# Token-major v made once per layer by whole 128x128 transposes, and the outputs' products grouped by array shape, in the RWKV mixers of a four-layer network

## The chip, the cores and the metric

The kernel runs on one core of one Trainium2 chip. The metric is the device time of one execution in microseconds (us).

## What is computed

Four layers in a row on 512 latent tokens of 1024 channels; the first two carry 256 context tokens along. Each of the first two layers projects its normalised input and gives the parts to three mixers: an RWKV mixer (4 heads of 64 channels, run over the tokens forwards and backwards), a short convolution and differential attention. The last two layers, attention and a gated recurrence, each with a feed-forward part, are not touched here. The RWKV part of the reference, cut:

```python
def rwkv_scan(state0, terms, reverse, with_output):
    def step(S, inp):
        w_t, k_t, v_t, a_t, b_t = inp[-5:]
        sa = jnp.einsum('bhvk,bhk->bhv', S, a_t)
        S = S * w_t[:, :, None, :] + sa[..., None] * b_t[:, :, None, :] + v_t[..., None] * k_t[:, :, None, :]
        y_t = jnp.einsum('bhvk,bhk->bhv', S, inp[0]) if with_output else None
        return S, y_t
...
    for d, reverse in ((0, False), (1, True)):
        s_ctx, y_c = rwkv_scan(state0, tc, reverse, need_ctx_out)
        _, y_l = rwkv_scan(s_ctx, tl, reverse, True)
```

`need_ctx_out` holds in the first layer only.

## The kernel before

The RWKV scan is done in chunks of 64 tokens. `layer` calls `rw_stage` six times per layer: three blocks of 256 tokens (context first) for each of two directions `d`. One stage, in the order of the code:

1. It loads its slices of keys, r and (in `rw_vt`) v from DRAM, where the projections left them channel-major.
2. *Preparation*: decay and rate from two small products with `wup` (L528), a scan and exponentials on ScalarE and VectorE, then the tiles `G` and `AR`; the in-chunk products `AS` (L584), masked by VectorE; the transposes `GT` of `G` (L595).
3. `rw_vt` turns v token-major, 16 blocks of 64x64: even heads' blocks by TensorE's transpose mode, odd heads' as plain float32 products with the identity (L504; a plain float32 product shows as two instructions in the trace, a transpose as one, so a stage has 24).
4. The diagonal blocks of the chunk matrices are inverted: `AS` goes through DRAM into a layout of one block per partition, VectorE does 15 serial steps (L613 to L617, tiles `X`, `tt`), and the result returns through DRAM into `D` and `DT` by 16 small transfers (L627). Then `txA` (L636, tile `tx`), a mask into `W` (L637), and three rounds of `tx` products (L645) with an addition each give `TT`.
5. *Chunks*: for each of four chunks, `zp` from `AS`, `UV` and the running state (L664 and L666), copied to `zs`; `up` from `TT` and `zs` (L673), copied into `UV`; `sp` from `GT` and `UV` (L681), from which VectorE makes the next state (L686, L687); and the output `yp`, for each of four heads one product with `UV` (L695, all 128 rows and 64 columns of the array, written 128*64 below) and one with the state (L697, 64*64). `UV` holds v and `up` stacked.

The projections that are still missing (`proj`, products L324) have no tie to the stages and stand between them. The Tile scheduler sets the order on each engine when the program is built, from its own estimates of durations; each engine then works through its list in order. Most of a stage's tiles have one buffer (`rb` = 1: `G`, `X`, `D`, `DT`, `W`, `vt`), those of the chunks two (`cb` = 2: `AR`, `AS`, `GT`, `TT`, `UV`). The two stages of one block of the order (d = 0, then d = 1) are prepared close together, so that there are three *pairs* of stages per layer. A *burst of v* below is one stage's L504 group.

Of the kernel before, what the change touches and what calls it, by code (L numbers as in the profile page):

```python
# [19 lines left out]
P = 128  # L20
# [29 lines left out]
# ---------------------------------------------------------------- host layout  # L50
# [105 lines left out]
def _wt(w, nk=8):  # L156
    """[K, N] -> [N/128, K/(128*nk) pieces, 128, nk, 128]"""
    K, N = w.shape
    return np.ascontiguousarray(w.reshape(K // (P * nk), nk, P, N // P, P).transpose(3, 0, 2, 1, 4))


def prep(inputs):
# [4 lines left out]
    # [l, nblk 6, 128, 8, 512]  # L167
# [11 lines left out]
    # f(rel) = rb[rel + 383]; table row p, column m: rel = p - m + 384  # L179
# [3 lines left out]
    g = np.stack([a["rg_w_a_2"][0], a["rg_w_i_2"][0]], 1)  # [blk, 2, 256, 256]  # L183
    o["rgg"] = np.ascontiguousarray(g.reshape(4, 2, 2, P, 256).transpose(0, 3, 1, 2, 4))  # blk, p, gate, kc, col
# [30 lines left out]
# ---------------------------------------------------------------- kernel  # L215
class Kern:
    def __init__(self, es, tc, ins, out, dbg=None, upto=99):
# [11 lines left out]
        # a load that the following weight loads queue up behind  # L229
        self.behind = self.last_load = None  # L230
        # GpSimd takes the low parts of every so many weights (0: of none)
# [19 lines left out]
    def mm(self):  # L251
        """a bank of products: of self.pm, or of two pools in turn"""
        pool, n = self.pm, self.nmm
        if self.mms:
            pool, n = self.mms[self.nmms % len(self.mms)]
            self.nmms += 1
        return self.t(pool, [P, 512], "mm", n)

    # ---- persistent state
# [24 lines left out]
    # ---- weights  # L284
    def load_w(self, src, nk=8, ncol=P, keep=None):
        """src: dram AP [128, nk, ncol] -> (hi, lo) float32r tiles; keep: (pool, number) of tiles apart from the rolling ones"""
# [16 lines left out]
    def split(self, hi, lo, src, eng=None):  # L303
        """hi + lo = src, both float32r"""
# [3 lines left out]
    def put_split(self, dst, cols, src, hi):  # L308
        """high and low part of src to dram; hi: scratch; src is overwritten"""
# [5 lines left out]
    def gemm(self, ps, wl, mov, total=None):  # L315
        """ps: list of psum APs, wl: list of (hi, lo, nk); mov: list (per psum) of function kc -> (hi, lo)"""
# [16 lines left out]
    def order(self, later, first):  # L333
        """first before later in their engine's queue"""
        self.tc.add_manual_dep(later.ins, first.ins.name, mybir.DependencyInfo(mybir.DependencyClass.NoSync, mybir.DependencyReason.DATA), reason="order")

    # ---- reciprocal square roots
    def rsqrt_cols(self, pool, src, n, eps=None, floor=None):
        """1 / sqrt(src + eps) of [128, n] (n small): bit-level seed and three Newton steps"""
# [15 lines left out]
    def log_tables(self):  # L355
        """the tables of rsqrt_act (and of Exp, Square, Copy, Identity), ahead of its first use"""
        self.tc.keep_in_program_order(self.nc.scalar.preload_act_table_set("natural_log_exp_and_others"))

    def rsqrt_act(self, pool, src, n, eps=EPS, half=False):
        """1 / sqrt(src + eps) of [128, n] (n small, eps: number or [128, n]): seed from the logarithm and one Newton step"""  # L360
# [20 lines left out]
    def tok_sum(self, ps, sqs, n, hold=None):  # L381
        """ps[token, b] = sum over channels (partitions, and the tiles of sqs) of token block b; hold: so many columns of later products come first"""
# [7 lines left out]
    def tok_sum2(self, st, sq, i):  # L390
        """as tok_sum, one tile after the other; only the very first product has the start flag, which clears the whole bank"""
# [10 lines left out]
    def bcast(self, pool, ps, cols, nb):  # L402
        """ps[:, token] (psum, nb * 128 columns) = cols[token, block] on every partition"""
# [7 lines left out]
    def heads_bcast(self, pool, ps, cols):  # L411
        """ps[channel, token] of one 128-channel chunk = cols[token, head of the channel]"""
# [5 lines left out]
    # ---------------------------------------------------------------- rwkv  # L418
    def rw_alloc(self, l, es):
        """tiles and small per-partition coefficients of one layer's rwkv mixer"""  # L420
# [3 lines left out]
        for n in ("r", "v", "m0", "m1", "ks0", "ks1", "ys0", "ys1"):  # L424
            R[n] = self.dp.tile([P, 2, T], F32, tag=f"rw{n}_{l}", name=f"rw{n}_{l}", bufs=1)
        R["lw"] = self.t(rp, [P, T], "lw")
# [5 lines left out]
        # 0:4 w0/2, 4:8 a0/2, 8:10 kk0, 10:12 kk1, 12:14 al(k), 14:16 be(k), 16:18 alpha0, 18:20 beta0, 20:22 alpha1, 22:24 beta1  # L432
# [9 lines left out]
        # slot 0: even rows k, odd rows b (alpha = beta = -0.5, negated) ; slot 1 the other way round  # L442
# [4 lines left out]
        # static buffers of the block inverses  # L447
# [16 lines left out]
    def rw_keys(self, l, ks, st):  # L464
        """m0 = [k even ; kk odd], m1 = [kk even ; k odd]; ks: sbuf tiles of k per channel chunk"""
# [27 lines left out]
    def rw_vt(self, tb):  # L493
        """token-major v of one token block: even heads in rows 0:64, odd heads in rows 64:128"""
        nc, R, rp = self.nc, self.R, self.rp
        ident = self.c("ident")
        ps = self.t(self.pa, [P, 8, 64], "ax", self.nax)
        vt = self.t(rp, [P, 8, 64], "vt", self.rb)
        vl = self.rw_load("v", tb, 1)
        for c in range(4):  # L500
            for hp in range(2):
                for e in range(2):
                    h = slice(e * 64, e * 64 + 64)
                    nc.tensor.matmul(ps[h, c * 2 + hp, :], lhsT=vl[h, hp, c * 64:c * 64 + 64], rhs=ident[h, h],  # L504
                                     start=True, stop=True, is_transpose=e == 0)
        nc.scalar.copy(out=vt, in_=ps)
        return vt

    def rw_stage(self, l, d, st, with_y):
# [10 lines left out]
        rl = self.rw_load("r", tb, 1) if with_y else None  # L520

        # decay and in-context rate
# [1655 lines left out]
```

## Time and profile before

| | |
|---|---|
| runs shown | 2908.32, 2912.96, 2920.25 us (median 2912.96) |
| profiled execution, first to last instruction | 2921.2 us |
| TensorE busy | 2677.0 us (92%) |
| VectorE, ScalarE, GpSimd busy | 1528.2, 1034.2, 743.2 us |
| the two RWKV mixers, by the places of their stages' products | 146 to 492 us, and 991 to 1355 us |

TensorE is busy most of the time, but its matmuls overlap: one that shows 0.22 us can begin 0.04 us after the one before it. What a group costs is therefore read from where it begins and where the next group begins, not from its busy time. `PEclk` is the granted clock of TensorE in a stretch, as a share of 2.4 GHz; at 0.50 it is at its lower level, 1.2 GHz, throughout.

### The profile page before, as it was taken

To read this page: it belongs to the slowest core of one execution; us is meant where nothing else is said; L and a number is where in the kernel's file an instruction comes from. 1 tells how busy PE (TensorE), PEld (TensorE's weight loads), DVE (VectorE), ACT (ScalarE), POOL (GpSimd) and SP (SyncE) were. 2 spreads that over 40 slices of the span, in tenths; PEclk is the share of its full clock that TensorE was granted. 3 is DMA by queue.
4 is the path that set the end of the run, shared out by engine and by line. 5 is a ranking of instruction groups with operands and counts; after the bars stand their busy time and mean duration, and the time that the engine had idled before them with its cause. 6 is when DMAs were issued, how large, how long until landed. Compare 5 with 4: busy or idle time off the path is not lost.

```text
span 2921.2 us, 42875 instructions
## 1 busy us (share of the span) xinstructions
PE 2677.0 (92%) x16938; PEld 2171.6 (74%) x16938; DVE 1528.2 (52%) x2925; ACT 1034.2 (35%) x1946; POOL 743.2 (25%) x631
## 2 busy tenths in 40 slices
PE   5999999969988999999898999799999987999998
PEld 2877777756687766666667888698888876988886
DVE  7264553517644366464375666665443487654423
ACT  4231222216534222122254445543222356432221
POOL 2310111414445121112122325431110254411101
PEclk8988979978798878889789999899999998999999
DMA  5332223466232322224643111022223311222232
GB/s 200 124 98 56 57 77 106 145 177 187 89 130 86 103 68 66 77 72 133 195 129 112 44 62 51 22 73 94 94 94 93 99 55 65 87 94 95 94 99 74
DMA packets 173785, 283.31 MB, mean 97 GB/s; under 512 B 53648, under 2 KB 110864, under 8 KB 173584
## 3 DMA queue, kind: packets, MB, share of 16 engines
q1 hardware_dynamic: 173584, 280.58, 31.0%
q8 instruction: 133, 2.18, 0.3%
q14 instruction: 68, 0.56, 0.1%
HBM read 235.68 MB, written 44.83 MB: 96 GB/s over the span
## 4 chain that ended last, share of the span: by engine, by line
PE 57%; DVE 13%; ACT 5%; issue 4%; POOL 3%; DMA 3%; SPq 0%; POOLq 0%; ACTq 0%; DVEq 0%
PE mm L324 14%; PE mm L1495 7%; PE mm L1458 5%; PE mm L1456 5%; PE mm L1459 5%; PE mm L1562 2%; PE s L1149 2%; PE s L1148 2%; DVE tt L616 1%; POOL wlo L300 1%; PE po L1194 1%; ACT whi L297 1%; PE ax L504 1%; PE tx L645 1%; PE yp L697 1%
## 5 line engine op out<-in xcount | busy, mean ns | idle before, releaser
L297 ACT CAST whi<-wraw 128x1024 fp32r<-128x1024 f32 (+2 forms) x311 | 318.2, 1026 | 702.3 <-PE mm L1458 281.1
L300 POOL TENSOR_TENSOR wlo<-wraw,whi 128x1024 fp32r<-128x1024 f32 (+1 forms) x122 | 292.9, 2403 | 830.4 <-ACT whi L297 753.8
L1458 PEld LDWEIGHTS mm<-hlo,whi 128*128 128x128 f32 x1632 | 311.8, 191 | 75.1
L1456 PE MATMUL mm<-hhi,whi 128*128 128x512 f32 x816 | 330.1, 404 | 9.5 <-ACT whi L297 9.5
L324 PE MATMUL mm<-hhi,whi 128*128 128x512 f32 (+1 forms) x992 | 331.2, 370 | 3.9 <-ACT whi L297 2.1
L1459 PE MATMUL mm<-hhi,wlo 128*128 128x512 f32 x816 | 327.1, 401 | 6.2 <-POOL wlo L300 6.2
L1458 PE MATMUL mm<-hlo,whi 128*128 128x256 f32 x1632 | 330.2, 284 | 0.0
L324 PE MATMUL mm<-hlo,whi 128*128 128x512 f32 (+1 forms) x992 | 327.6, 365 | 0.5 <-POOL hlo L843 0.5
L300 DVE TENSOR_TENSOR wlo<-wraw,whi 128x1024 fp32r<-128x1024 f32 (+1 forms) x189 | 235.0, 1246 | 177.3 <-ACT whi L297 173.8
L324 PE MATMUL mm<-hhi,wlo 128*128 128x512 f32 (+1 forms) x992 | 322.6, 363 | 0.0
L324 PEld LDWEIGHTS mm<-hhi,whi 128*128 128x128 f32 x992 | 186.3, 204 | 39.0 <-issue 3.9
L324 PEld LDWEIGHTS mm<-hlo,whi 128*128 128x128 f32 x992 | 186.6, 204 | 28.7 <-issue 4.8
L324 PEld LDWEIGHTS mm<-hhi,wlo 128*128 128x128 f32 x992 | 184.9, 204 | 25.4 <-issue 3.3
L1456 PEld LDWEIGHTS mm<-hhi,whi 128*128 128x128 f32 x816 | 156.0, 191 | 14.5 <-ACT whi L297 11.6
L1459 PEld LDWEIGHTS mm<-hhi,wlo 128*128 128x128 f32 x816 | 157.8, 194 | 7.4 <-POOL wlo L300 7.3
L2029 POOL TENSOR_TENSOR g<-g,rsb 128x512 f32<-128x512 f32 x44 | 56.6, 1287 | 397.9 <-DVE g L2028 397.9
L1152 DVE TENSOR_REDUCE mx<-s 128x1 f32<-128x768 f32 (+1 forms) x80 | 67.2, 848 | 81.4 <-PE s L1149 81.0
L1495 PE MATMUL mm<-yhi,whi 128*128 128x256 f32 (+1 forms) x280 | 93.6, 336 | 12.3 <-ACT whi L297 10.5
L1524 POOL TENSOR_TENSOR acc<-acc,sq 128x256 f32<-128x256 f32 x48 | 51.9, 1085 | 195.2 <-ACT sq L1522 195.2
L1154 ACT ACTIVATE p<-s,mx 128x768 f32<-128x768 f32 (+1 forms) x80 | 65.0, 813 | 98.1 <-DVE mx L1152 84.4
L1495 PE MATMUL mm<-yhi,wlo 128*128 128x256 f32 (+1 forms) x280 | 91.8, 329 | 0.0
L1495 PE MATMUL mm<-ylo,whi 128*128 128x256 f32 (+1 forms) x280 | 91.9, 328 | 0.0
(426 smaller groups left out, 5986.3 us busy)
## 6 DMA issues: line engine op xcount, KB each, us to landing
wraw<-in_win_dram SPq DMA_DIRECT2D x76, 512.0 KB, 3.5
wraw<-in_modw_dram SPq DMA_DIRECT2D x48, 512.0 KB, 4.5
wraw<-in_fg_dram SPq DMA_DIRECT2D x44, 512.0 KB, 3.3
wraw<-in_fu_dram SPq DMA_DIRECT2D x44, 512.0 KB, 3.2
wraw<-in_fd_dram SPq DMA_DIRECT2D x32, 512.0 KB, 3.6
wraw<-in_wout_dram SPq DMA_DIRECT2D x24, 512.0 KB, 3.4
wraw<-in_wv_dram SPq DMA_DIRECT2D x16, 512.0 KB, 3.3
wraw<-in_rgin_dram SPq DMA_DIRECT2D x16, 512.0 KB, 3.3
```

The source lines that it names most:

```text
L297: nc.scalar.copy(out=hi, in_=raw)
L300: (nc.gpsimd if pool else nc.vector).tensor_tensor(out=lo, in0=raw, in1=hi.bitcast(F32), op=ALU.subtract)
L324: mm = nc.tensor.matmul(pp, lhsT=w[:, k, :], rhs=mv(kc)[sel], start=(kc == 0 and w is hi and sel == 0), stop=(kc == tot - 1 and w is lo))
L1148: nc.tensor.matmul(s[:, a:b], lhsT=qs[:, q], rhs=kd[:, k0 + a:k0 + b], start=True, stop=False)
L1149: nc.tensor.matmul(s[:, a:b], lhsT=qs[r, q], rhs=H["kl"][r, k0 + a:k0 + b], start=False, stop=True)
L1152: nc.vector.tensor_reduce(out=mx, in_=s, axis=AX.X, op=ALU.max, negate=True)
L1154: nc.scalar.activation(e[:, 0:nk], s, AF.Exp, bias=mx, accum_out=sm)
L1456: self.nc.tensor.matmul(ps, lhsT=w[0][:, kc, :], rhs=hi[:, kc, :], start=kc == 0, stop=False)
L1458: self.nc.tensor.matmul(ps[:, q], lhsT=w[0][:, kc, :], rhs=lo[i][kc], start=False, stop=False)
L1459: self.nc.tensor.matmul(ps, lhsT=w[1][:, kc, :], rhs=hi[:, kc, :], start=False, stop=kc == KC - 1)
L1495: self.nc.tensor.matmul(p_, lhsT=a[:, k, :], rhs=mov(kc, s)[b], start=kc == 0 and i == 0, stop=kc == n - 1 and i == 2)
L1562: nc.tensor.matmul(p_[:, s], lhsT=a[:, kc, :], rhs=b(kc), start=kc == 0 and i == 0, stop=kc == 7 and i == 2)
```

## The change

`rw_vt` is now called once per layer and pair of heads, right after v's projection, on the whole 768 tokens: GpSimd makes a copy `x` of v with neighbouring chunks of 64 tokens swapped, TensorE transposes v and `x` in blocks of 128x128, so that for either head of the pair one of the two blocks has its tokens in the right rows, and ScalarE and VectorE pick these out. The result goes to DRAM (`R["vt"]`), and each stage loads its slice. In the chunks the output's four state products follow `zp`'s products, and its four `UV` products stand together behind `sp`'s; all add into one bank, of which only the first product of each half has the start flag (`y_add`, with an order of that product before the others). Comments and docstrings are dropped too; nothing else differs.

```diff
+        R["vt"] = self.dp.tile([P, 2, 3, 4, 64], F32, tag=f"rwvt_{l}", name=f"rwvt_{l}", bufs=1)
...
-    def rw_vt(self, tb):
...
-        ps = self.t(self.pa, [P, 8, 64], "ax", self.nax)
-        vt = self.t(rp, [P, 8, 64], "vt", self.rb)
-        vl = self.rw_load("v", tb, 1)
-        for c in range(4):
-            for hp in range(2):
-                for e in range(2):
-                    h = slice(e * 64, e * 64 + 64)
-                    nc.tensor.matmul(ps[h, c * 2 + hp, :], lhsT=vl[h, hp, c * 64:c * 64 + 64], rhs=ident[h, h],
-                                     start=True, stop=True, is_transpose=e == 0)
-        nc.scalar.copy(out=vt, in_=ps)
-        return vt
+    def rw_vt(self, hp, v, t, x):
+        nc, R = self.nc, self.R
+        nc.gpsimd.tensor_copy(out=x.rearrange("p (t a b) -> p t a b", a=2, b=64), in_=v.rearrange("p (t a b) -> p t a b", a=2, b=64)[:, :, ::-1, :])
+        vt = t.rearrange("p (t c n) -> p t c n", c=4, n=64)
+        for tb in range(3):
+            ps = self.t(self.pa, [P, 2, 2, P], "ax", self.nax)
+            for b in range(2):
+                for i, s in enumerate((v, x)):
+                    nc.tensor.transpose(ps[:, b, i, :], s[:, tb * 256 + b * P:tb * 256 + b * P + P], self.c("ident"))
+            o = vt[:, tb].rearrange("p (b x) n -> p b x n", x=2)
+            nc.scalar.copy(out=o[0:64], in_=ps[0:64, :, :, 0:64])
+            for j in range(2):
+                nc.vector.tensor_copy(out=o[64:P, :, 1 - j, :], in_=ps[64:P, :, j, 64:P])
+        nc.sync.dma_start(out=R["vt"][:, hp], in_=vt)
...
+        vt = self.t(rp, [P, 2, 4, 64], "vt", self.rb)
+        nc.sync.dma_start(out=vt, in_=R["vt"][:, :, tb])
...
-        vt = self.rw_vt(tb)
...
+            if with_y and S0 is not None:
+                for hp in range(2):
+                    for e in range(2):
+                        h = slice(e * 64, e * 64 + 64)
+                        y_add(hp, e, c, S0[h, hp, :], AR[h, hp * 4 + c, 1, :])
             zs = self.t(rp, [P, 2, 64], "zs", 2)
...
             if with_y:
                 for hp in range(2):
                     for e in range(2):
-                        h = slice(e * 64, e * 64 + 64)
-                        nc.tensor.matmul(yp[h, hp, c, :], lhsT=UV[:, c, hp, e, :], rhs=AS[:, c, hp, e, 64:128], start=True, stop=S0 is None)
-                        if S0 is not None:
-                            nc.tensor.matmul(yp[h, hp, c, :], lhsT=S0[h, hp, :], rhs=AR[h, hp * 4 + c, 1, :], start=False, stop=True)
+                        y_add(hp, e, c, UV[:, c, hp, e, :], AS[:, c, hp, e, 64:128])
...
+                    if n == "v":
+                        self.rw_vt(hp, s, ST(), ST())
```

The first place is TensorE's list in a chunk of the first stage of layer 0, before. L695 is an output product with `UV`, L697 one with the state, L681 `sp`, L664 and L666 the next chunk's `zp`, L324 a projection.

```order
L695 MATMUL yp_1336<-AS_1125,UV_1333 64x64
L697 MATMUL yp_1336<-AR_1109,state_239_1356 64x64
L681 MATMUL cx_1380<-UV_1333,GT_1150 64x64 x4
L695 MATMUL yp_1336<-AS_1125,UV_1333 64x64
L697 MATMUL yp_1336<-AR_1109,state_239_1356 64x64
L695 MATMUL yp_1336<-AS_1125,UV_1333 64x64
L697 MATMUL yp_1336<-AR_1109,state_239_1356 64x64
L695 MATMUL yp_1336<-AS_1125,UV_1333 64x64
L697 MATMUL yp_1336<-AR_1109,state_239_1356 64x64
L324 MATMUL mm_3701<-hlo_113,whi_3696 128x256
L324 MATMUL mm_3700<-hhi_112,wlo_3697 128x512
L664 MATMUL cx_1397<-UV_1333,AS_1125 64x64
```

The same list a chunk further on, with the change. L665 is `y_add`, L692 `up`, L700 `sp`, L677 and L679 `zp`, L648 the next stage's `tx`.

```order
L677 MATMUL cx_1435<-UV_1371,AS_1184 64x64
L679 MATMUL cx_1435<-state_252_1427,AR_1168 64x64
L665 MATMUL yp_1374<-AR_1168,state_252_1427 64x64 x4
L648 MATMUL tx_1685<-DT_109_494,W_1666 64x64
L692 MATMUL cx_1450<-zs_1448,TT_1353 64x64 x4
L648 MATMUL tx_1685<-DT_109_494,W_1666 64x64 x6
L665 MATMUL yp_1374<-AS_1184,UV_1371 64x64
L648 MATMUL tx_1685<-DT_109_494,W_1666 64x64 x4
L700 MATMUL cx_1457<-UV_1371,GT_1209 64x64 x4
L665 MATMUL yp_1374<-AS_1184,UV_1371 64x64 x3
L648 MATMUL tx_1685<-DT_109_494,W_1666 64x64 x5
```

The two kinds of output products no longer alternate: the state's four follow `zp` in its shape, and three of the other four follow `sp` in its shape; one still stands alone ahead of `sp`.

The second place is TensorE's list where the second stage of layer 0 is prepared, before: `GT`'s transposes (L595), the burst of v (L504), then the next stage's products with `wup` (L528).

```order
L595 MATMUL ax_1547<-con_3_59,G_1498 128x128 x4
L504 MATMUL ax_1553<-con_3_59,lv_1555 64x64 x16
L528 MATMUL ax_1866<-lw_476,wup_478 128x256
L324 MATMUL mm_3577<-hlo_113,whi_3572 128x256
L324 MATMUL mm_3576<-hhi_112,wlo_3573 128x512
```

The same place with the change (`GT` is L599, `wup` L532), and ahead of the first stage the new transposes (L504), among the last projections that the first stage needs:

```order
L599 MATMUL ax_1587<-con_3_59,G_1538 128x128 x4
L532 MATMUL ax_1887<-lw_477,wup_479 128x256
L324 MATMUL mm_3520<-hhi_112,whi_3515 128x256
L324 MATMUL mm_3519<-hlo_113,whi_3515 128x512
```

```order
L324 MATMUL mm_1056<-hhi_112,whi_1052 128x512
L504 MATMUL ax_1024<-con_3_59,st_1022 128x128
L504 MATMUL ax_1024<-con_3_59,st_961 128x128
L504 MATMUL ax_1024<-con_3_59,st_1022 128x128
L504 MATMUL ax_1032<-con_3_59,st_1022 128x128
L504 MATMUL ax_1032<-con_3_59,st_961 128x128
L504 MATMUL ax_1032<-con_3_59,st_1022 128x128
L324 MATMUL mm_1057<-hhi_112,whi_1052 128x256
```

Each stage's burst is gone, and twelve transposes for each pair of heads (24 per layer) stand ahead of the first stage.

The third place is the list of SyncE, which issues the transfers, ahead of the first inversion (`scr`) of layer 0, with the change. Each stage's `vt` waits for its one buffer, that is for ScalarE's two copies of the stage before it into `UV`.

```order
L524 DMA vt_1143<-rwvt_476 128x2x256
...
L524 DMA vt_1514<-rwvt_476 128x2x256
...
L524 DMA vt_1885<-rwvt_476 128x2x256
L289 DMA wraw_3695<-in_win_dram 128x1024
L609 DMA scr_1222<-AS_1184 16x8x16
```

Before, one load of v (`lv`) stood ahead of the first `scr` transfer there, and the two next ones behind its eight parts; now three loads do.

## Rows read from the trace of the kernel before

**Rows 1.** The page's first part: busy time by engine, share, instructions.

```profile
PE 2677.0 (92%) x16938; PEld 2171.6 (74%) x16938; DVE 1528.2 (52%) x2925; ACT 1034.2 (35%) x1946; POOL 743.2 (25%) x631
```

**Rows 2.** Windows, layer 0: chunks and preparations in turn; layer 1: one chunk stretch.

```profile
core 0: us, PE busy (x) PEld busy (x) DVE busy (x) ACT busy (x) POOL busy (x), PEclk, DMA share, GB/s
217.00:275.00 58.00, 56.06 (x670) 41.01 (x668) 24.18 (x49) 11.54 (x27) 4.83 (x3) 0.90 0.19 49
275.00:322.00 47.00, 43.45 (x270) 33.63 (x271) 35.42 (x90) 13.13 (x24) 6.71 (x4) 0.83 0.24 65
322.00:386.00 64.00, 63.73 (x699) 46.98 (x700) 22.64 (x48) 10.82 (x27) 2.46 (x2) 0.85 0.17 45
386.00:433.00 47.00, 41.40 (x265) 32.89 (x262) 35.19 (x88) 11.43 (x19) 9.01 (x4) 0.83 0.32 88
1180.00:1251.00 71.00, 70.33 (x698) 49.91 (x699) 23.44 (x52) 15.20 (x34) 6.65 (x4) 0.77 0.21 60
```

**Rows 3.** Timeline, TensorE and VectorE, where a preparation ends: start, duration, work.

```profile
317.42 0.51 PE L324 MATMUL mm<-hhi,whi 128*128 128x512 f32 x2
317.76 0.51 PE L324 MATMUL mm<-hlo,whi 128*128 128x512 f32 x2
321.82 1.98 PE L645 MATMUL tx<-DT,W 64*64 64x64 f32 x32 [3.55 <-DVE W L637]
...
321.09 0.67 DVE L637 TENSOR_TENSOR W<-tx,con 128x512 f32<-128x512 f32 x1
```

**Rows 4.** Groups of instructions by line, both mixers.

```profile
L697 PE MATMUL yp<-AR,state 64*64 64x64 f32 x304 | 53.5, 260 | 0.0
L504 PE MATMUL ax<-con,lv 64*64 64x64 f32 x288 | 48.0, 266 | 1.0 <-DVE AS L586 1.0
```

**Rows 5.** Timeline, TensorE, one chunk of the first stage.

```profile
231.74 0.33 PE L695 MATMUL yp<-AS,UV 128*64 128x64 f32 x2
232.00 0.33 PE L697 MATMUL yp<-AR,state 64*64 64x64 f32 x2
232.25 0.45 PE L681 MATMUL cx<-UV,GT 128*64 128x64 f32 x8
232.54 0.28 PE L695 MATMUL yp<-AS,UV 128*64 128x64 f32 x2
...
234.03 0.39 PE L324 MATMUL mm<-hlo,whi 128*128 128x256 f32 x1
```

**Rows 6.** Timeline, TensorE, the chunk ahead of it, which has no state products.

```profile
228.09 0.45 PE L681 MATMUL cx<-UV,GT 128*64 128x64 f32 x8
228.37 0.40 PE L695 MATMUL yp<-AS,UV 128*64 128x64 f32 x6
228.71 0.39 PE L324 MATMUL mm<-hhi,whi 128*128 128x256 f32 x1
...
229.26 0.34 PE L664 MATMUL cx<-UV,AS 64*64 64x64 f32 x4
...
229.92 0.38 PE L324 MATMUL mm<-hlo,whi 128*128 128x256 f32 x1
```

**Rows 7.** Timeline, TensorE, the end of the second stage's products in layer 0.

```profile
189.91 0.60 PE L595 MATMUL ax<-con,G 128*128 128x128 f32 x4
190.44 3.49 PE L504 MATMUL ax<-con,lv 64*64 64x64 f32 x24
```

**Rows 8.** Timeline, VectorE, the state of the chunk of rows 5.

```profile
233.08 0.29 DVE L687 TENSOR_TENSOR state<-sm,plast 128x128 f32<-128x128 f32 x1
```

**Rows 9.** Tile D: its transfers' issue (min/median/max ns) and their time to landing.

```profile
L627 SPq DMA_DIRECT2D D<-scrb x96: 302/429/1648, 203.2 to 1304.6; - x96
...
DMA to landing us min/median/max: 1.5/1.8/4.4
```

**Rows 10.** Windows around a burst of v.

```profile
183.00:195.00 12.00, 10.58 (x80) 7.92 (x76) 10.28 (x26) 2.90 (x7) 2.31 (x1) 0.99 0.38 115
195.00:205.00 10.00, 10.00 (x27) 7.09 (x27) 5.62 (x13) 4.06 (x9) 0.00 (x0) 0.50 0.24 60
```

More of the change, by code (lines that the diff above doesn't have):

```diff
@@ L491, in rw_load @@
         return t
-    def rw_vt(self, tb):
-        nc, R, rp = self.nc, self.R, self.rp
-        ident = self.c("ident")
-        ps = self.t(self.pa, [P, 8, 64], "ax", self.nax)
-        vt = self.t(rp, [P, 8, 64], "vt", self.rb)
-        vl = self.rw_load("v", tb, 1)
-        for c in range(4):
-            for hp in range(2):
-                for e in range(2):
-                    h = slice(e * 64, e * 64 + 64)
-                    nc.tensor.matmul(ps[h, c * 2 + hp, :], lhsT=vl[h, hp, c * 64:c * 64 + 64], rhs=ident[h, h],
-                                     start=True, stop=True, is_transpose=e == 0)
-        nc.scalar.copy(out=vt, in_=ps)
-        return vt
+    def rw_vt(self, hp, v, t, x):
[12 more added lines that the diff above has]
+        nc.sync.dma_start(out=R["vt"][:, hp], in_=vt)
     def rw_stage(self, l, d, st, with_y):
@@ L653, in rw_stage, with y_add @@
             h = slice(e * 64, e * 64 + 64)
-            nc.scalar.copy(out=UV[h, :, :, e, :].rearrange("p c a n -> p (c a) n"), in_=vt[h])
+            nc.scalar.copy(out=UV[h, :, :, e, :], in_=vt[h].rearrange("p a c n -> p c a n"))
         yp = self.t(pa, [P, 2, 4, 64], "yp", 1) if with_y else None
+        begun = {}
+        def y_add(hp, e, c, lhsT, rhs):
+            mm = nc.tensor.matmul(yp[e * 64:e * 64 + 64, hp, c, :], lhsT=lhsT, rhs=rhs, start=e not in begun, stop=True, skip_group_check=True)
+            if e in begun:
+                self.order(mm, begun[e])
+            else:
+                begun[e] = mm
         for c in (range(4) if d == 0 else range(3, -1, -1)):
```

## The prediction

> **What bounds the kernel now.** I read the page's first part, then windows over the mixers cut where the work changes its kind, then single instructions. TensorE is busy 92% of the span [rows 1], so the first guess is that a removed product is removed time. The windows show two kinds of stretch [rows 2]. In the chunks (217 to 275, 322 to 386 and 1180 to 1251 us) TensorE is busy all but 0.3 to 2 us of 58 to 71 us: there it is the bound. In the preparations (275 to 322, 386 to 433 us) it is idle 3.6 and 5.6 us of 47, and the VectorE column is the one that is high (35 us). What ends them is seen in [rows 3]: TensorE has done its projections at 318 us and waits 3.55 us for `W`, which VectorE writes at 321.09, straight behind the 15 steps of the second stage's inversion, since its list is in order. So from the second stage's `wup` products to the first stage's `W` a chain of VectorE and transfers sets the length, some 46 us in each of six pairs, and a product removed there buys only a longer wait, unless other work of TensorE is put in its place.
>
> **What the change removes and adds.** *The outputs.* The state's output products show 304 instructions [rows 4], 8 for a chunk, so 38 chunks have them. In such a chunk the two shapes alternate: from 231.74 to 234.03 us, less 0.29 us of `sp` between, the 16 instructions take 2.00 us, and each change of shape opens a new block of about 0.26 us that holds just two [rows 5]. Where the shape stays, eight of `sp` and six output products begin within 0.62 us, 0.044 us each, and the 16 of `zp` within 0.66 us, 0.041 us each, with the change at their end [rows 6]. With the change the eight state instructions follow `zp` in its shape (0.33 us), six of the others follow `sp` in its shape (0.26 us), and two stay alone ahead of `sp`, one block of 0.26 us. That is 0.85 us; I take 0.95, since the group behind `zp` sometimes meets another shape. Saved: 2.00 - 0.95 = 1.05 us, times 38 is **40 us**, all of it in the chunks, where TensorE is the bound. The Trainium skill (TensorEngine Tiling (Array Packing), Instruction Overhead) says that each matmul has some 60 cycles of overhead, so that one of a single column takes as long as one of 60. By that alone the 64-column products here would cost the same in whatever order they stand, and this part of the gain would be nothing. The same page's Key Properties say that a change of tiling mode drains the engine; the trace bears out this one, with 0.125 us each in [rows 5] and 0.044 us in [rows 6].
>
> *The bursts of v.* One burst of 24 instructions takes 3.49 us [rows 7], and 288 of them [rows 4] make twelve: 42 us of TensorE. Six belong to a pair's first stage and delay the second stage's `wup`, which starts the chain: 21 us on the path. The other six, 21 us, stand inside the preparations, where they fill time in which TensorE would wait. There it counts what the scheduler puts in their place. By the two orders, between the second stage's last `GT` transpose and the end of its wait for `D` there are 4608, 6400 and 4864 more projection columns in the three pairs of layer 0 and 8192, 2816 and 2816 more in layer 1, 29,696 in all; the total of projections up to the last output product is about what it was (240,128 columns for 243,968 in layer 0, 261,376 for 258,560 in layer 1), so these are taken out of the chunks. 768 columns take 0.34 us [rows 3], so 13 us of projections leave the stretches in which TensorE is the bound for stretches in which it waits. A pair's share is 1.2 to 3.6 us, and the burst's 3.5 us and the idle time (3.6 and 5.6 us) hold it. Gain: **13 us** of these 21; if the moved columns lengthen the chain, 0, if the chain itself is shortened, up to 21.
>
> *The new transposes.* 48 of 128x128. The nearest row has four `GT` transposes in 0.53 us, change of shape included [rows 7], 0.13 us each: **6 us** more of TensorE, ahead of the first stage. GpSimd's copies of v (four of 128x768), 12 copies of ScalarE and 24 of VectorE replace 12 copies of ScalarE; they stand under projections that no stage needs, and the result is first read by `UV`, which is needed only after `TT`, some 60 us later. If that cover were gone, a store and a load in a row, at 1.8 us each to landing [rows 9], and some 3 us of copies would stand on the path in each layer, 13 us.
>
> *The queues.* SyncE issues as many loads as before, `vt` for `lv`, and two stores per layer more. But in layer 0 three `vt` loads now stand ahead of the first `scr` transfers, each waiting for ScalarE's copies of the stage before. Behind them in the list are the inversion's transfers and a weight. ScalarE in turn holds these copies at its head until `vt` lands; behind them are `GT`'s copies and the casts of weights that the projections wait for. I put two landings and an issue on the path once per layer (4 us each, rounded down to 3 as the projections are loaded ahead): **6 us**; from below nothing, from above the bound in the rivals.
>
> *New waits.* The outputs were also cover. From `sp` (232.25) to the state's end (233.37) it takes 1.12 us [rows 5, 8], and TensorE came to the next chunk's `zp` only after 234.03, so 0.7 us of the time between was more than needed. With 1.3 us of outputs gone there and a third to a half of it refilled by projections, about 0.2 us a chunk becomes a wait: **8 us** in 38. Between `up` and `sp` little changes, between `zp` and `up` the state's products take the place of projections. In layer 0 the order puts the second stage's `txA` one chunk earlier in two pairs; `D` can only be rewritten when the first stage's `txA` is done, and eight transfers of 0.43 us and 1.8 us to landing [rows 9] then take 5.3 us, of which I count 2 us as uncovered, twice: **4 us**.
>
> **The sum.** 40 + 21 + 13 - 6 - 6 - 8 - 4 = 50 us at full clock. The stretches have granted clocks of 0.77 to 0.90 [rows 2], and work at 0.5 costs double; at 0.85 a removed microsecond is worth about 1.1, so 55 us. The profiled execution spans 2921.2 us and is the upper end of the runs shown, whose median is 2913, so from the span 2866 and for the median **2858 us**, 1.9% faster. What is beyond the mixers stays: from the last projections of layer 1 on, TensorE's list is the same, instruction by instruction.
>
> **The rivals.**
> *The clock rises.* After the burst of v at 190 to 194 us the clock goes from 0.99 to 0.50 and stays there for 10 us [rows 10]; it is no proof, as `wup`'s products stand there too. If the falls in the chunks go with the bursts and the clock comes to 0.97 there, then 58 us at 0.90, 64 at 0.85 and 71 at 0.77 shrink by 4, 8 and 15 us, 27 us, for half of the six stretches; with some for the others the gain is 55 + 35 = 90 us: about 2823. Against it: a longer wait at `W` also stands ahead of a fall (to 0.83 in both preparations).
> *The chain takes it.* If the chunks are bound by the round from `zp` over ScalarE and VectorE to the next state as soon as the outputs shrink, half of the 40 us becomes waits, and the 13 us don't come: 55 - 20 - 13 = 22 to 30 us, about 2887. For it speaks the single buffer of `W`, `D` and `DT`; against it that the two directions' chunks, the next pair's preparation and projections stand between.
> *Whole transposes keep the clock low.* Here, TensorE would go to 0.50 around the new transposes, which lie close together twice per layer; a fall of 10 us [rows 10] costs 5 us, four make 20 us, and the time would be about 2878. For the burst of v, a third of whose instructions were transposes, [rows 10] would bear it out; `GT`'s eight transposes stand in the stretch at 0.99, against it. The Trainium skill (TensorE: Matmul & The Clock Gate, PE-mode transpose) says that transposes don't count as busy for the clock; no row here shows transposes alone.
> *Slower: the heads of the queues.* If in each stage `vt`'s landing holds ScalarE, and by it the casts of weights, until TensorE has no projection left, each stage loses a landing and an issue, then the cast and what follows. To come out slower by over 0.5% (15 us) this must eat the 55 us as well, 70 us, or 5.8 us in each of the twelve stages, more than the longest landing (4.4 us) [rows 9] without any cover: about 2930. Against it: after the first pair the copies wait for a load issued tens of us ahead.
>
> **How the numbers follow.** Chances: as summed 0.47; the clock rises 0.2; the chain takes it 0.18; whole transposes keep the clock low 0.08; slower 0.04; nearly nothing, all the waits at their upper ends together, 0.03. The likeliest is 2858. The range reaches from 2815, somewhat under the clock's case, to 2890, just over the chain's, and leaves out deeper falls and the last two. A measurement here tells about 0.5%, 15 us, from no change. Faster by more: the first four but for a tenth of the chain's, 0.9; within: 0.06; slower: 0.04.
>
> **What would show it.** The L504 group falls to 48 instructions of about 0.13 us from one to the next. `y_add` shows 624 instructions, and a chunk of them begins within 0.95 us instead of 2.0. The waits of `tx` for `W` stay, 3 to 6 us a pair. The chunk stretches shrink by 8 to 13 us each and stay nearly fully busy; from the last mixer on the two traces are the same. I am wrong if TensorE's idle time in the chunks grows by more than 15 us, if ScalarE's waits for `vt` hold the casts, or if the clock in the chunks moves by more than 0.05.

## The result and the profile after

The changed kernel takes 2807.8 us (median of 4 runs, 2801.0 to 2819.75) where the kernel before takes 2916.6 on the same chip: ratio 0.9624, 95% interval 0.9595 to 0.9653. That is 109 us, twice the 55 of the forecast, and outside the forecast's range.

The profiled execution of the changed kernel spans 2805.6 us with a mean granted clock of 0.933; that of before 2921.2 us with 0.909. The first line is the page's, busy time by engine, and answers to [rows 1]:

```profile
PE 2540.6 (91%) x16698; PEld 2078.3 (74%) x16698; DVE 1529.9 (55%) x2949; ACT 1033.3 (37%) x1946; POOL 745.0 (27%) x635
```

TensorE's busy time falls by 136 us, with 240 instructions fewer of 16,938. Span less busy time, its idle time, rises from 244 to 265 us. The windows, cut at the same events as [rows 2] (chunks, preparation, chunks, preparation of layer 0, and the second chunk stretch of layer 1):

```profile
core 0: us, PE busy (x) PEld busy (x) DVE busy (x) ACT busy (x) POOL busy (x), PEclk, DMA share, GB/s
222.90:265.10 42.20, 40.73 (x633) 31.06 (x632) 18.49 (x37) 9.01 (x23) 2.48 (x2) 1.00 0.21 52
265.10:313.20 48.10, 44.27 (x269) 33.97 (x267) 39.72 (x100) 14.68 (x27) 9.11 (x5) 0.82 0.34 92
313.20:353.80 40.60, 40.04 (x616) 30.97 (x617) 16.60 (x38) 7.72 (x21) 0.11 (x1) 0.96 0.15 36
353.80:396.50 42.70, 38.05 (x292) 30.46 (x291) 38.10 (x95) 12.83 (x23) 10.92 (x5) 0.96 0.39 109
1110.80:1154.30 43.50, 43.06 (x607) 31.37 (x607) 19.45 (x42) 12.98 (x28) 7.95 (x5) 0.94 0.33 96
```

The three chunk stretches of [rows 2] go from 193 to 126 us, and their clock from 0.90, 0.85 and 0.77 to 1.00, 0.96 and 0.94. Of the two preparations shown, one takes 1 us more and the other 4 to 5 us less. To tell work from clock, a length is split in two: length times clock (what it would be at 2.4 GHz throughout) and the rest, "for the clock". It is an accounting, not yet a cause: a wait counts for the clock too if the clock is low in it, and not all work takes twice as long there (a burst of v that lies wholly at 1.2 GHz, at 1043.6 us before, takes 5.12 us where others take 3.42). For the three chunk stretches it gives 161 to 122 us of work and 32 to 4 us for the clock. For the whole span, cut at the same instructions in both traces, with the time at 1.2 GHz from the records of the clock:

| stretch (how many) | length, us | at 1.2 GHz, us | at full clock |
|---|---|---|---|
| start to the first `wup` product | 146.2 → 154.7 | 23.9 → 23.9 | +8.5 |
| first stage's `wup` to the second's (2) | 61.4 → 42.8 | 24.4 → 6.8 | -9.8 |
| preparations, to the first `tx` with `W` (6) | 294.0 → 277.8 | 108.3 → 58.1 | +8.9 |
| chunk stretches (6) | 354.1 → 261.6 | 85.8 → 17.0 | -58.1 |
| last output to the attention's scores (2) | 226.5 → 219.8 | 35.5 → 32.9 | -5.4 |
| attention of layer 0 to the next `wup` | 348.2 → 361.8 | 111.3 → 115.3 | +11.6 |
| the rest | 1479.6 → 1475.8 | 131.2 → 111.2 | +6.2 |
| sum | 2909.9 → 2794.3 | 520 → 365 | -38 |

So 38 us of the 116 between these two executions are work, and 78 (half of 155 us at 1.2 GHz) are the clock; the means of all runs, in the table of the experiments, give 45 and 60. The forecast had 50 and 5. Ten of the 78 us lie in the last row, where TensorE's list is the same as before, and aren't explained: the time at 1.2 GHz also differs between two executions of one kernel (over the whole span 376 us in this one of the change, 334 us in that of `after_same` below).

The groups by line answer to [rows 4]; L504 is now the new transposes:

```profile
L665 PE MATMUL yp<-AS,UV 128*64 128x64 f32 x320 | 28.8, 229 | 0.1
L665 PE MATMUL yp<-AR,state 64*64 64x64 f32 x304 | 17.3, 230 | 0.0
L504 PE MATMUL ax<-con,st 128*128 128x128 f32 x48 | 8.5, 286 | 5.5 <-POOL st L498 5.5
```

The outputs with the state went from 53.5 to 17.3 us of busy time. A chunk's timeline (TensorE: start, duration, work) shows how, beside [rows 5]:

```profile
239.89 0.33 PE L665 MATMUL yp<-AS,UV 128*64 128x64 f32 x2
240.15 0.45 PE L648 MATMUL tx<-DT,W 64*64 64x64 f32 x8
240.53 0.45 PE L700 MATMUL cx<-UV,GT 128*64 128x64 f32 x8
240.81 0.40 PE L665 MATMUL yp<-AS,UV 128*64 128x64 f32 x6
241.14 0.56 PE L648 MATMUL tx<-DT,W 64*64 64x64 f32 x10
```

The lone pair opens a block of 0.26 us, as the forecast took it, and the six behind `sp` take 0.33, where it counted 0.26.

Five of the things that TensorE waited for, over all stages (total, times, longest), with the change:

```profile
PE tx L648 <- DVE W L640: 17.1, 5, 7.0
PE ax L504 <- POOL st L498: 5.5, 4, 1.4
PE cx L679 <- DVE state L706: 2.7, 3, 1.1
PE cx L692 <- ACT zs L687: 2.3, 11, 0.2
PE tx L639 <- DMA D<-scrb: 1.6, 4, 0.6
```

### The profile page after: what moved, and what is told of

Its sections match the earlier page's. It is cut to its first block, busy times and chain, and to the rows that moved or that the text cites. A ratio compares the mean times of both kernels' runs of the same rounds, so it can differ in the third digit from the quotient of the medians.

```text
span 2805.6 us, 42446 instructions
## 1 busy us (share of the span) xinstructions
PE 2540.6 (91%) x16698; PEld 2078.3 (74%) x16698; DVE 1529.9 (55%) x2949; ACT 1033.3 (37%) x1946; POOL 745.0 (27%) x635
## 4 chain that ended last, share of the span: by engine, by line
PE 35%; DVE 8%; ACT 4%; POOL 2%; issue 2%; DMA 2%; SPq 0%; POOLq 0%; ACTq 0%; DVEq 0%
PE mm L1513 6%; PE mm L1476 6%; PE mm L1474 6%; PE mm L1477 5%; PE mm L324 4%; PE mm L1580 2%; PE s L1167 1%; ACT whi L297 1%; PE s L1166 1%; PE z L1816 1%; DVE wl L306 1%; DVE wlo L300 1%; DVE xc L2092 1%; DVE w L1852 1%; PE po L1212 1%
## 5 line engine op out<-in xcount | busy, mean ns | idle before, releaser
L1476 PEld LDWEIGHTS mm<-hlo,whi 128*128 128x128 f32 x1632 | 309.7, 190 | 73.8
L324 PE MATMUL mm<-hhi,whi 128*128 128x512 f32 (+1 forms) x992 | 327.4, 364 | 11.2 <-DVE st L1018 4.3
L324 PE MATMUL mm<-hlo,whi 128*128 128x512 f32 (+1 forms) x992 | 318.1, 358 | 0.5 <-POOL hlo L859 0.5
L324 PE MATMUL mm<-hhi,wlo 128*128 128x512 f32 (+1 forms) x992 | 316.9, 357 | 0.0
L324 PEld LDWEIGHTS mm<-hhi,whi 128*128 128x128 f32 x992 | 183.5, 200 | 45.0 <-DVE st L1018 5.0
L324 PEld LDWEIGHTS mm<-hhi,wlo 128*128 128x128 f32 x992 | 180.9, 199 | 26.8 <-issue 4.7
L324 PEld LDWEIGHTS mm<-hlo,whi 128*128 128x128 f32 x992 | 181.4, 199 | 24.4 <-issue 2.7
L2049 DVE SCALAR_TENSOR_TENSOR th<-mm,g 128x512 f32<-128x512 f32 x44 | 30.4, 691 | 115.2 <-PE mm L1477 107.1
```

Source lines behind the costliest of these rows:

```text
L324: mm = nc.tensor.matmul(pp, lhsT=w[:, k, :], rhs=mv(kc)[sel], start=(kc == 0 and w is hi and sel == 0), stop=(kc == tot - 1 and w is lo))
L1476: self.nc.tensor.matmul(ps[:, q], lhsT=w[0][:, kc, :], rhs=lo[i][kc], start=False, stop=False)
```

## The experiments

One table holds all results. The ratio is to the kernel before, run on the same chip; "work" and "clock" are span times clock and span times (1 - clock), means over the timed runs. Before has 2661 to 2662 and 249 to 251 us in three sets of runs; work repeats to 5 us or better, and nearly all the spread between runs of one kernel is clock (before: 2906.35 us at 0.917, 2924.24 at 0.910).

| kernel | v | outputs | median, us | ratio, 95% interval | work | clock |
|---|---|---|---|---|---|---|
| before | alternating burst | alternating | 2910 to 2917 | | 2662 | 250 |
| the change | once per layer | grouped | 2807.8 | 0.9624 [0.9595, 0.9653] | 2617 | 190 |
| the same again, `after_same` | once per layer | grouped | 2795.3 | 0.9600 [0.9571, 0.9630] | 2622 | 173 |
| `v_only` | once per layer | alternating | 2837.3 | 0.9743 [0.9710, 0.9776] | 2652 | 186 |
| `y_only` | alternating burst | grouped | 2861.6 | 0.9817 [0.9775, 0.9859] | 2628 | 232 |
| `y_end` | alternating burst | grouped, at the end | 2870.0 | 0.9853 [0.9827, 0.9878] | 2636 | 232 |
| `burst_grouped` | burst by kind | alternating | 2861.5 | 0.9811 [0.9775, 0.9848] | 2664 | 197 |
| `burst_plain` | burst, all plain | alternating | 2839.0 | 0.9742 [0.9714, 0.9771] | 2655 | 183 |
| `no_burst` | none | alternating | 2849.4 | 0.9784 [0.9746, 0.9822] | 2637 | 213 |
| `y_burst_grouped` | burst by kind | grouped | 2797.5 | 0.9601 [0.9576, 0.9625] | 2620 | 175 |
| `y_burst_plain` | burst, all plain | grouped | 2791.6 | 0.9589 [0.9558, 0.9620] | 2620 | 172 |
| `y_no_burst` | none | grouped | 2786.8 | 0.9574 [0.9541, 0.9607] | 2605 | 183 |
| `after_alt` | the change + alternating burst | grouped | 2843.5 | 0.9759 [0.9730, 0.9787] | 2639 | 202 |
| `after_grp` | the change + burst by kind | grouped | 2806.6 | 0.9641 [0.9610, 0.9672] | 2636 | 170 |

**The theories.** A: the burst of v alternates between transpose mode and plain products, and such alternation, not the products, is what costs time and brings the clock down. B: less work and fewer waits shorten the chain, and the clock follows by chance or by less small work. C: the whole 128x128 transposes made ahead are themselves what is better.

### The two parts alone

`v_only` is the change with the outputs of before; `y_only` is before with the changed outputs (`y_add`).

> The new token-major v with the old, alternating outputs. The change as a whole took 109 us of the median, and 156 us less of its span lie at half clock (378 us against 534), worth some 78 us. Theory: the falls of the clock came with the bursts of v, so this part alone brings the clock back: about 60 us faster than before, under 430 us at half clock. Rival (the clock fell with the alternating outputs): about 25 us faster, over 490 us at half clock.

> The grouped outputs with the old bursts of v in every stage. Theory (falls come with the bursts): the 40 us of the outputs alone, 40 to 48 us faster, half clock 480 us or more. Rival (falls come with the alternating outputs): 70 us faster or more, half clock under 430 us. If the round to the next state takes the place of the outputs: under 25 us.

Measured: 73 us of gain for v and 49 for the outputs, 121 together, where the whole has 109 and, in a second set, 118. The parts add nearly. They are of different kinds: the outputs save 33 us of work and 19 of clock, v 9 us of work and 65 of clock. `v_only` has 387 us at 1.2 GHz, as the theory wanted it; `y_only` has 451, between the theory's 480 or more and the rival's under 430, so the alternating outputs had a part in the low clock too.

### The burst in another order, and no burst

`burst_grouped` is the kernel before with one loop moved outwards, so that a burst has its eight transposes (`e == 0`) first and its eight plain products behind them:

```diff
-        for c in range(4):
-            for hp in range(2):
-                for e in range(2):
+        for e in range(2):
+            for c in range(4):
+                for hp in range(2):
```

`no_burst` leaves the turning of v out: ScalarE copies the channel-major slice into `vt`, so the mixers work on wrong values of v.

```diff
-        ps = self.t(self.pa, [P, 8, 64], "ax", self.nax)
...
-        for c in range(4):
-            for hp in range(2):
-                for e in range(2):
-                    h = slice(e * 64, e * 64 + 64)
-                    nc.tensor.matmul(ps[h, c * 2 + hp, :], lhsT=vl[h, hp, c * 64:c * 64 + 64], rhs=ident[h, h],
-                                     start=True, stop=True, is_transpose=e == 0)
-        nc.scalar.copy(out=vt, in_=ps)
+        nc.scalar.copy(out=vt.rearrange("p a n -> p (a n)"), in_=vl.rearrange("p a n -> p (a n)"))
```

> Before, with the loops of each burst of v in another order: the eight products in transpose mode first, then the eight plain ones, instead of in turn. If each change between the two modes costs as a change of shape does, a burst falls from 3.5 us to 1.2 to 1.6 us, and the kernel is 15 to 35 us faster (25 us of TensorE and part of the clock). If the products are slow by themselves (0.145 us each), the burst stays at 3.5 us and the time within 6 us of before.

> Before with the bursts left out: ScalarE copies the loaded channel-major v to where the token-major one belongs, so the outputs are of wrong values of v. Against v_only it tells what the new transposes ahead of the first stage cost: theory 6 to 10 us more gain than v_only (68 us faster than before); rival, seen in the trace of the change (the stretches ahead of the first stage 8.5 and 13.7 us longer): 20 us more than v_only.

Measured: the loop order alone gives 49 us, with the same instructions, more than the 15 to 35 expected. The timeline of `burst_grouped` at the second stage (TensorE, the place of [rows 7]) has the burst's 24 instructions in 1.63 us, from the first to the product behind it:

```profile
186.09 1.70 PE L504 MATMUL ax<-con,lv 64*64 64x64 f32 x24
187.72 0.70 PE L528 MATMUL ax<-lw,wup 64*128 64x256 f32 x2
```

Before it is 3.42 us:

```profile
163.27 3.49 PE L504 MATMUL ax<-con,lv 64*64 64x64 f32 x24
166.69 0.70 PE L528 MATMUL ax<-lw,wup 64*128 64x256 f32 x2
```

Twelve times 1.8 us are 21 us of TensorE, but the table's work doesn't fall (2662 to 2664): these microseconds became waits, and TensorE's idle time rises from 244 to 262 us. The whole gain is the clock, 250 to 197, and theory B, which needs less small work or fewer waits, has neither here. Windows of the 6 us behind the bursts (columns as in the windows above) show it. Before, four of the twelve:

```profile
166.70:172.70 6.00, 6.00 (x22) 3.72 (x21) 1.80 (x3) 3.28 (x7) 0.00 (x0) 0.56 0.39 123
193.90:199.90 6.00, 6.00 (x17) 3.78 (x17) 2.18 (x4) 3.54 (x7) 0.00 (x0) 0.57 0.16 45
296.40:302.40 6.00, 6.00 (x17) 4.00 (x16) 1.87 (x3) 5.00 (x9) 0.00 (x0) 0.56 0.31 80
...
1273.20:1279.20 6.00, 6.00 (x25) 5.17 (x25) 0.00 (x0) 3.67 (x6) 0.09 (x1) 0.72 0.30 67
```

All twelve lie between 0.50 and 0.72. By the records of the clock, two of them were low ahead of the burst already (from 1037.9 and from 1222.2 us); at the ten others the fall begins in the burst or within 1.3 us of its end. In `burst_grouped` ten of twelve are at 1.00; the two others stand in chunk stretches, where the clock was down ahead of the burst already (0.52 and 0.50 in the 10 us before it). Four of them, the first three the same bursts as above:

```profile
165.90:171.90 6.00, 6.00 (x32) 3.94 (x31) 2.48 (x5) 4.25 (x10) 0.00 (x0) 1.00 0.55 149
187.70:193.70 6.00, 6.00 (x29) 4.13 (x28) 4.90 (x10) 5.06 (x10) 0.00 (x0) 1.00 0.31 77
274.80:280.80 6.00, 6.00 (x25) 3.78 (x25) 3.20 (x6) 5.82 (x12) 0.79 (x1) 1.00 0.34 83
353.80:359.80 6.00, 6.00 (x33) 3.76 (x32) 0.58 (x2) 2.18 (x4) 0.00 (x0) 0.50 0.18 57
```

`no_burst` has 25 us less work than before, 15 less than `v_only` (2637 against 2652): this is what the new transposes and their copies and waits cost, for which the forecast counted 12 (6 for transposes, 6 for queues). Its time missed both expectations: it was to gain 6 to 20 us more than `v_only` and gains 12 us less. It has more time for the clock, 213 against 186; with the old outputs and no alternating bursts that time differs from kernel to kernel (table: 183 to 213), and why is open.

### Both orders, and the state's products at the end

`y_burst_grouped` has the loop order above and the changed outputs, and not the new way of v. `y_end` is `y_only` with the state's four products moved from behind `zp` to behind the other four (against the kernel before, cut):

```diff
                 for hp in range(2):
                     for e in range(2):
+                        y_add(hp, e, c, UV[:, c, hp, e, :], AS[:, c, hp, e, 64:128])
+            if with_y and S0 is not None:
+                for hp in range(2):
+                    for e in range(2):
                         h = slice(e * 64, e * 64 + 64)
...
+                        y_add(hp, e, c, S0[h, hp, :], AR[h, hp * 4 + c, 1, :])
```

> The kernel before with the grouped outputs and with each burst of v in the order of its two kinds (eight transposes, then eight plain products); the new way of v is left out. If alternation is what both parts of the change remove, the two gains add: 49 us of the grouped outputs and 49 us of the grouped burst, about 2812 us against 2910 of the kernel before, some 10 us above the whole change or level with it, half clock below 400 us of the span, chunk stretches together below 290 us. If the two share the same falls of the clock, 2830 or more. If the token-major v made once per layer has a worth of its own, this stays 15 us or more above 2808.

> The grouped outputs alone, with the state's four products at the chunk's end behind the other four, rather than behind zp. If the grouping is what counts, nearly the 49 us of the grouped outputs, 2861 to 2872 us. If moving the state's products ahead, under the wait for zs, is what counts, most of the gain goes: 2885 us or more.

Measured: `y_burst_grouped` takes 2797.5 us, 14 less than expected and level with the change (ratios 0.9601 against 0.9624 and 0.9600), whose 24 whole transposes per layer it lacks: theory C falls. `y_end` keeps 42 of the 49 us: what counts is the grouping. The place behind `zp` is worth 8 us of work, 0.2 us in each of 38 chunks; that this is one more change of shape is likely by its size, but not shown.

### A burst added back

The changed kernel with a burst per stage of 16 products on the keys' tile, the result unused; alternating in `after_alt`, by kind in `after_grp`:

```diff
+        px = self.t(self.pa, [P, 8, 64], "ax", self.nax)
+        vl = ml[0]
+        for c in range(4):
+            for hp in range(2):
+                for e in range(2):
+                    h = slice(e * 64, e * 64 + 64)
+                    nc.tensor.matmul(px[h, c * 2 + hp, :], lhsT=vl[h, hp, c * 64:c * 64 + 64], rhs=self.c("ident")[h, h],
+                                     start=True, stop=True, is_transpose=e == 0)
+        nc.scalar.copy(out=self.t(rp, [P, 8], "dum", 1), in_=px[:, :, 0])
```

> The changed kernel with one burst per stage added that computes nothing of use: 16 products of 64x64 on the keys' tile, in the alternating order of the burst of before, and a copy of one column of each. If alternation brings the clock down, the falls return: half clock 480 us or more of the span (378 in the changed kernel), a burst takes about 3.5 us, and the time is 60 to 75 us above the changed kernel, about 2875. If only the burst's own time counts, 12 times 3.5 us, half of it hidden in the preparations: 2830 to 2850 us, half clock about 390.

> The same added burst with its eight transposes first and its eight plain products behind them. If alternation is the cause, a burst takes about 1.7 us, half clock stays at 380 to 410 us and the time is 10 to 25 us above the changed kernel, 2818 to 2833. If it is the presence of small products in two kinds, whatever their order, as after_alt.

Measured: alternating is 37 us above by kind (2843.5 against 2806.6, same chip), 32 of them clock. By kind is 5 to 12 us above the change, by the ratios to before of its two sets, at or below the lower end of the 10 to 25 expected: of the 20 us that twelve bursts take (1.64 us each) 14 to 19 show in the work, and the clock gives 3 to 20 back. The falls return: in `after_alt` the 6 us behind the burst lie at 0.50 to 0.72 in eleven of twelve, in `after_grp` all twelve at 1.00. One window of each, behind the second stage's burst of layer 0, `after_alt` first:

```profile
196.80:202.80 6.00, 6.00 (x15) 3.79 (x15) 1.51 (x4) 2.51 (x6) 0.00 (x0) 0.50 0.18 57
```

```profile
193.00:199.00 6.00, 6.00 (x31) 4.54 (x30) 4.12 (x10) 3.63 (x8) 0.00 (x0) 1.00 0.25 72
```

The size missed: 60 to 75 us and at least 480 us at 1.2 GHz were expected of `after_alt`, and 2843.5 us with 409 us at 1.2 GHz came. By these two numbers alone the rival, that only the burst's own time counts (2830 to 2850 us, about 390), fits better. What decides against it is the pair: the work of the two is nearly the same (2639 and 2636), and the clock (202 and 170) and the falls behind the bursts differ. These falls are shorter than before: within the 20 us behind the bursts 101 us in all lie at 1.2 GHz, where before it was 143. Why they are shorter isn't shown.

### All products plain

`burst_plain` is the kernel before with one argument dropped, so that all 16 products are plain and a burst has 32 instructions; heads, halves of the array and loop order stay. `y_burst_plain` adds the changed outputs, `y_no_burst` is `no_burst` with them, and `after_same` is the change again on their chip.

```diff
-                                     start=True, stop=True, is_transpose=e == 0)
+                                     start=True, stop=True)
```

> The changed kernel itself, on the chip of the three below. 2800 to 2812 us against about 2911 of before. If the once-per-layer transposes have a worth beyond the removed alternation, it is faster than y_burst_plain by 10 us or more; if they have none, level with it or slower.

> The kernel before with all 16 products of the burst plain float32 ones (32 instructions where there were 24), in the old loop order; no transpose mode. If changing between the two kinds is the price, a burst takes 1.4 to 1.9 us, no fall of the clock begins within 3 us of it, and the time is that of the burst grouped by kind, 2855 to 2870 us. If the price is that of small products between two halves of the array (the heads still alternate), a burst takes 3.5 us or more and the time stays at 2900 or above.

> The same with the grouped outputs. By alternation of kinds 2795 to 2812 us; by halves of the array 2860.

> The grouped outputs, and no v turned on TensorE at all: ScalarE copies the channel-major v into its place, so that the values are wrong and only the time counts. It bounds what any way of turning v can give: if the grouped burst is nearly free, 2785 to 2800 us; if twelve bursts of 1.7 us count in full, 20 us under y_burst_plain; if TensorE's waits take all of it, level with it.

Measured: 32 plain instructions take less than 24 of two kinds. The timeline of `burst_plain`, first a burst at full clock, then the one of the place above, in part of which the clock is at 0.50:

```profile
289.42 1.15 PE L504 MATMUL ax<-con,lv 64*64 64x64 f32 x32
290.50 0.70 PE L528 MATMUL ax<-lw,wup 64*128 64x256 f32 x2
...
186.75 1.52 PE L504 MATMUL ax<-con,lv 64*64 64x64 f32 x32
188.20 0.70 PE L528 MATMUL ax<-lw,wup 64*128 64x256 f32 x2
```

The three whole bursts at full clock take 1.08 us from the first to what follows, 0.034 us an instruction. The price of a change of kind is best read from the same instructions in two orders: 3.42 us with 15 changes and 1.63 with one are some 0.13 us for a change. The halves of the array alternate here as before, and the falls are gone: 1.00 behind eleven of twelve bursts, the twelfth at 0.50 among the chunks, where the clock was down ahead of the burst (0.60 in the 10 us before it). The second burst, and that one:

```profile
188.20:194.20 6.00, 6.00 (x31) 4.14 (x28) 2.61 (x6) 4.83 (x10) 0.00 (x0) 1.00 0.28 76
260.40:266.40 6.00, 6.00 (x30) 3.74 (x29) 0.66 (x3) 2.61 (x5) 0.00 (x0) 0.50 0.20 60
```

In `y_burst_plain` all twelve are at 1.00. Dropping the one argument gives 75 us, as much as the new way of v. It is some 20 us faster than `burst_grouped`, which wasn't expected: 10 us in work (0.55 us less in each of twelve bursts are 7 of them) and 14 in the clock. The 0.55 us come from the order of the halves and not from the missing transposes: by the starts in the traces, the transposes of `burst_grouped` begin 0.056 us apart and its plain products, all in one half, 0.117 us (two instructions); in `burst_plain`, where the halves alternate, a plain product begins every 0.058 us.

`y_burst_plain`, `after_same` and `y_no_burst` are level, 2791.6, 2795.3 and 2786.8 us, with intervals that overlap. No version beats the change measurably, and even a v turned for nothing would not: `y_no_burst` has 15 us less work than `y_burst_plain`, and 11 us more go to the clock.

## Why the prediction was wrong

**The step that failed** is the last factor: "The stretches have granted clocks of 0.77 to 0.90, and work at 0.5 costs double; at 0.85 a removed microsecond is worth about 1.1, so 55 us." It takes the clock as a property of the stretch, to be multiplied with; it was in the main an effect of the very products removed. Five us were counted for it, 60 to 77 measured (table of experiments: 250 to 190 and 173). Theory A's evidence is `burst_grouped`, `burst_plain` and the pair `after_alt`/`after_grp`: the falls come with alternation in a burst and go without it, with as many products or more. It isn't without exception: behind one burst of twelve in `y_only`, in `y_end` and in `after_alt` no fall comes. The trace of before had shown it: [rows 10] was read as "no proof", because `wup`'s products stand there too, but all twelve bursts have such a window, and in `burst_grouped` `wup`'s products still follow the burst, at 1.00. The forecast's own sign of being wrong, a clock in the chunks that moves by more than 0.05, came: it moved by 0.10, 0.11 and 0.17. The rival "the clock rises" named the mechanism, with a chance of 0.2. Its 35 us are what the chunk stretches gave (69 us less at 1.2 GHz, half of it); its sum of 90 us was too low, since it saw falls only there: the preparations gave up 50 us at 1.2 GHz too, and the stretches ahead of them 18 (table).

**Outputs, 40 us.** Right: 33 us of work in `y_only`, where 8 of new waits were to come off. The price of 0.26 us a block came back in the chunk shown above. By the Trainium skill (TensorEngine Tiling (Array Packing), Key Properties: a change of tiling mode drains the engine) order counts, and by its Instruction Overhead alone it wouldn't; the runs decide for the first, 33 us with the same products.

**Bursts of v, 21 + 13 us, less 6 and 6.** Mis-sized: 22 us net were counted, 9 measured (`v_only`'s work; 6 to 11 from `y_only` to the change). The columns of the projections moved as forecast: by the two traces the preparations have 29,696 more, 13 us, and 10 of these left the chunks, which have 58 us less work. But the preparations have 9 us more although six bursts left them: their room for "the burst's 3.5 us and the idle time" was not all free. And the stretches ahead of the first stages take 20 us more at full clock (8.5 and 11.6). Some 6 of these are projections that moved there from other stretches (14,080 columns); the rest, 14 us, is near the 15 by which `v_only` has more work than `no_burst`. 5.5 of it are TensorE's waits for GpSimd's copies, which the forecast put under cover.

**A chain sets the preparations, where "a product removed there buys only a longer wait".** Half right. At full clock they didn't shorten, as it said, and in `burst_grouped` the 21 us saved in the bursts became waits. But their clock rose, and that shortened them by 25 us.

**New waits, 18 us.** Idle time grew by 21 us, but in other places: 4.5 in the chunk stretches (3.6 to 8.1 us), 7 in the preparations (28.8 to 35.7), and the rest outside the stages. `zp` waited for the state 2.7 us in all, not 8, and `tx` for `D` 1.6. `vt` took 3.6 us to land at the median and held ScalarE 2.2 us in three stages.

**The other rivals.** *The chain takes it*: no, the chunk stretches shrank by 15 us each. *Whole transposes keep the clock low*: no; with the change the windows around those of layer 0 are at full clock, and so are those of layer 1 (925 to 955 us):

```profile
140.00:150.00 10.00, 9.07 (x55) 7.68 (x56) 1.84 (x7) 2.59 (x5) 1.61 (x3) 1.00 0.27 93
150.00:160.00 10.00, 8.62 (x45) 5.98 (x44) 3.90 (x11) 3.60 (x9) 2.42 (x2) 1.00 0.40 139
```

What the Trainium skill says behind it, that transposes don't count as busy for the clock in the same way (TensorE: Matmul & The Clock Gate, PE-mode transpose), decides nothing here: a burst by kind has as many transposes as an alternating one, and the falls go. *The heads of the queues*: no, by the 2.2 us in three stages above.

**What stays open**: why the clock falls behind alternating products. The runs show that it does, not whether the engine's slowness in the burst, the changes themselves or something beside them is what counts. Open too is why the time lost to the clock with the old outputs differs between `no_burst`, `v_only` and `burst_plain`, so that leaving the burst out altogether gains less than dropping its transpose mode (61 against 75 us).

## What to carry to other kernels

Where a window shows TensorE below its full clock, find what stands ahead of each fall, in all of them, before pricing a removal: if the removed products stand there, up to half of the time at 1.2 GHz may belong to them. Group small products by shape and by kind (transpose or plain) before building anything larger; here one dropped argument and one regrouped loop gave all that the larger change gave. Split each timed run into span times clock and the rest: the first repeats to a few us, and a gain in the second has another cause.

## What was not expected of the hardware

A change between a transpose-mode and a plain float32 product of 64x64 costs some 0.13 us, as long as two plain products take that alternate between the halves of the array (0.058 us each). A burst of 16 such alternating products, 3.4 us long, is followed by 3 to 20 us at 1.2 GHz within the next 20 in the kernel before, although TensorE is busy throughout (6.00 of 6.00 us in the windows above); in the order of kinds, or all plain, no fall starts within 3 us of its end. The order of the halves counts as well: plain products begin 0.058 us apart where the halves alternate, and 0.117 us where they stay in one. So grouping, which helped between kinds and between shapes, costs time between halves.
